# Memory projection first, squares of x summed by TensorE, no plain pair, and GpSimd for the lower parts of seven memory weight tiles

## The chip, the cores and the metric

The kernel runs on one core of a Trainium2 chip. The core's engines are TensorE (PE in the profile, its weight loads PEld), VectorE (DVE), ScalarE (ACT), GpSimd (POOL) and SyncE (SP), which here issues the DMA transfers. Each engine works through its own queue in order; semaphores tie the queues together. The metric is device time of one launch in microseconds, less is better.

## The reference

One layer of a decoder: an RMS norm of x, one combined projection, four groups of heads that mix over the tokens, and an output projection with a residual. 1,024 prompt tokens and 32 sample tokens are handled together (1,056 columns). Cut to what the change touches:

```python
def rmsnorm(x, g):
    xf = x.astype(jnp.float32)
    y = xf * lax.rsqrt(jnp.mean(xf * xf, axis=-1, keepdims=True) + EPS)
    return (y * g.astype(jnp.float32)).astype(x.dtype)

def memory_kv(mem, g_mem, w_mem_kv, g_mem_k):
    kv = rmsnorm(mem, g_mem) @ w_mem_kv          # 256 memory tokens, 2048 -> 1024
    k, v = jnp.split(kv, 2, axis=-1)
    k = rmsnorm(k.reshape(b, m, MEM_HEADS, MEM_HD), g_mem_k)
    return k, v.reshape(b, m, MEM_HEADS, MEM_HD)

hn = rmsnorm(x, g_norm)
proj = hn @ w_in                                 # group D's queries m_q among its columns
q = rmsnorm(m_q.reshape(b, L, MEM_HEADS, MEM_HD), g_mem_q)
s = jnp.einsum('blhd,bmhd->bhlm', q, mem_k) * (MEM_HD ** -0.5)
p = jax.nn.softmax(s, axis=-1)
o_mem = jnp.einsum('bhlm,bmhd->blhd', p, mem_v)
y_d = o_mem.reshape(b, L, GROUP_W) * jax.nn.silu(m_z)
```

## The kernel before

Everything is float32. A matmul with full accuracy is made of three matmuls on parts: an operand is split into an upper part (`wh`, `xh`: the value rounded to the type fp32r by a cast on ACT) and a lower part (`wl`, `xl`: value minus upper part, on DVE), and upper x upper, lower x upper and upper x lower are added in PSUM.

x lies transposed: 16 row tiles (k = 0 to 15) of 128 features by 1,056 tokens. The columns of `w_in` are 46 tiles of 128, taken two at a time as pairs. 44 of them (`ORDER`, L1708) are computed with one level of Strassen's scheme (`first_pair`, `second_pair`): seven products per pair, each of 24 matmuls of 264 columns, in two passes. Pass one works on row tiles 0 to 7, pass two on 8 to 15. The products are named by their x operand: B11, T2, B21, T1, T3, B22, T4 (`self.S`). Each operand is a difference or sum of four blocks of x (b11, b12 for row tiles 0 to 3, left and right half of the tokens; b21, b22 for 4 to 7), normalised first, split into two parts and kept for all pairs of the pass. `product` (L648) issues a product and asks `first_strands` (L432) for its operand as long as that does not stand; with every such step it also advances the projection of the memory (`memory`, L832) by one of its 16 steps. `make_weights` forms the seven weight operands of each pair on DVE and splits them. Results of pass one are written out and read back in pass two.

The remaining two tiles, Dq0 and Dq1 (queries of memory heads 0 and 1), are computed at the very start by `first_two` (L384) without that scheme: 16 x 2 x 3 x 3 = 288 matmuls of 352 columns on x times g, not yet normalised, since the norm is known only when all of x has come. `load_x` (L273) loads the 16 tiles, splits each (ACT L310, DVE L311), squares it on ACT (L289) and adds the squares up on DVE (L294). `row_norms` (L321) sums them over the features, takes the inverse root (`rsqrt`, some 13 small DVE operations in a chain) and spreads it over all partitions: R, by which the two tiles are multiplied (L415), and then x's blocks, together with g, in `first_strands` (`normal`, L440). GpSimd forms the lower parts of seven of the eight weight pieces of these tiles (L366).

`memory` loads the memory in two transfers and its weights in 16, splits them (ACT L881, DVE L882, two of 512 columns per step), and issues 12 matmuls of 512 columns per step (L902). Its last step feeds `memory_out`, which makes keys and values. The attention of a memory head (`d_head`, `d_unit`) is put into a queue of steps (`_Pipe`), of which `product` runs two ahead of each product's matmuls: heads 0 and 1 in pass one behind the first pair, 2 and 3 at the start of pass two.

Order on the engines is not the order of the source: the framework orders each engine's instructions, and a buffer of a pool is given again only when its last reader is done. So an engine's queue can wait for a buffer as well as for data.

Of the kernel before, what the change touches and what calls it, by code (L numbers as in the profile page):

```python
# [122 lines left out]
class _Step:  # L123
    def __init__(self, nc, tc, ctx, I, O):
# [148 lines left out]
    def load_x(self):  # L273
# [10 lines left out]
        self.x0, self.x0raw = block, raw  # L284

        def square(k, parts):
            sq = self.rtile("sq") if k < 8 else parts[2]
            for i, p in enumerate(parts[:2]):
                nc.scalar.activation(sq[:, i * H : i * H + H], p, AF.Square)  # L289
            i = int(k % 4 == 3)  # L290
            if self.acc[i] is None:
                self.acc[i] = sq
            else:
                nc.vector.tensor_tensor(self.acc[i], self.acc[i], sq, op=ALU.add)  # L294
        for k in range(KT):
            if k < 8:
                parts = [block(2 * (k // 4) + i, k % 4) for i in range(2)]
            else:
                xr = self.rtile("xr")
                parts = [xr[:, 0:H], xr[:, H:TOK], xr]  # L300
            if k < 8:
                for i in range(2):
                    nc.sync.dma_start(out=parts[i], in_=self.I["xT"][k, :, i * H : i * H + H])
            else:
                nc.sync.dma_start(out=parts[2], in_=self.I["xT"][k])
            hl = self.stile(F32R, "xhl")
            for i in range(2):
                h, l = (hl[:, x * TOK + i * H : x * TOK + i * H + H] for x in range(2))
                g = self.gn[:, k : k + 1]
                nc.scalar.activation(h, parts[i], AF.Copy, scale=g)  # L310
                nc.vector.scalar_tensor_tensor(l, parts[i], g, h.bitcast(F32), op0=ALU.mult,  # L311
                                               op1=ALU.subtract)
            self.xh[k], self.xl[k] = hl[:, 0:TOK], hl[:, TOK : 2 * TOK]
            if last:
                square(*last)
            last = k, parts
            if k == KT - 1:
                square(*last)
            yield k
# [1620 lines left out]
```

## Time and profile before

| what | value |
|---|---|
| median of 3 runs (lowest, highest) | 1568.07 us (1562.56, 1576.54) |
| the profiled execution | 1575.27 us |
| its span, first to last instruction | 1573.5 us |
| PE busy | 1530.4 us (97%) |
| DVE busy | 1105.2 us (70%) |
| ACT busy | 772.6 us (49%) |
| GpSimd busy | 23.3 us (1%) |
| mean granted TensorE clock | 0.985 |

The profile's tables give groups of instructions by line, engine, operation and tile names (output <- inputs), with shape and count, busy time, the mean duration of one in ns, and behind the bar the idle time ahead of them with what ended it. The timeline lists instructions in order of time, neighbours of one kind merged: start, duration, then in brackets how long the engine sat idle before and what it waited for. The chain of waits follows the work that ended last. Matmuls overlap: the duration of one is longer than the distance from its start to the next one's, so rates are taken from counts in a stretch.

### The profile page before, as it was taken

What the parts mean: (1) busy time and instruction counts of PE and PEld (TensorE: products, weight loads), DVE (VectorE), ACT (ScalarE), POOL (GpSimd) and SP (SyncE); (2) the same over time, 40 slices, a digit from 0 to 9 for tenths busy, and PEclk for the clock granted to TensorE, in tenths of its full rate; (3) what the DMA queues carried; (4) which work ended last, traced back from release to release, by engine and by line L of the source; (5) the groups of instructions that cost most, each with busy time, mean ns of one, the idle gap of its engine ahead of it and who ended that gap; (6) DMA issues with size and microseconds to landing.
All of it is one profiled execution on the core that took longest, in us unless ns stands there. A gap on an engine that the chain in (4) does not pass through costs nothing.

```text
span 1573.5 us, 30753 instructions
## 1 busy us (share of the span) xinstructions
PE 1530.4 (97%) x12194; PEld 1459.6 (93%) x12194; DVE 1105.2 (70%) x2283; ACT 772.6 (49%) x1620; POOL 23.3 (1%) x35
## 2 busy tenths in 40 slices
PE   7889999999999999999999999999998999999998
PEld 7668999999999999988998999999988999999998
DVE  8998645586555559665767776967779777596664
ACT  8466633322333336744468774645557443363332
POOL 3000000000000000000000000000000000000000
PEclk9899999999999999999999999999999999999999
DMA  7523222375332248158423333533437224587651
GB/s 272 193 92 109 69 103 94 142 267 193 109 110 100 95 148 308 62 144 298 139 78 84 109 90 121 173 123 90 167 119 244 82 104 168 188 288 267 209 203 63
DMA packets 102418, 236.77 MB, mean 150 GB/s; under 512 B 16516, under 2 KB 22532, under 8 KB 102276
## 3 DMA queue, kind: packets, MB, share of 16 engines
q1 hardware_dynamic: 102276, 234.82, 44.4%
q8 instruction: 96, 1.57, 0.4%
q14 instruction: 46, 0.38, 0.1%
HBM read 165.38 MB, written 69.41 MB: 149 GB/s over the span
## 4 chain that ended last, share of the span: by engine, by line
PE 75%; DVE 13%; ACT 5%; DMA 4%; issue 3%; SPq 0%; DVEq 0%; ACTq 0%
PE pj L668 64%; PE ms L902 2%; DVE wl L645 2%; DMA sx<-xs 1%; DVE s L430 1%; DVE xhl L311 1%; ACT wh L644 1%; ACT t L1280 1%; PE ms L1037 1%; DMA x<-in_xT 1%; ACT xhl L310 1%; DMA kc<-in_cache_mem_kT 1%; DVE t L1267 1%; PE ms L1313 1%; PE ms L1007 1%
## 5 line engine op out<-in xcount | busy, mean ns | idle before, releaser
L668 PE MATMUL pj<-s,wh 128*128 128x264 f32 x6720 | 1268.7, 288 | 7.6 <-ACT pj L751 5.5
L668 PEld LDWEIGHTS pj<-s,wh 128*128 128x128 f32 x6720 | 1055.5, 189 | 25.6 <-issue 12.7
L668 PE MATMUL pj<-s,wl 128*128 128x264 f32 x3360 | 960.3, 286 | 0.8 <-DVE wl L645 0.8
L668 PEld LDWEIGHTS pj<-s,wl 128*128 128x128 f32 x3360 | 636.7, 190 | 5.9 <-issue 4.1
L644 ACT CAST wh<-wr 128x512 fp32r<-128x512 f32 x300 | 186.3, 621 | 262.4 <-PE pj L668 248.3
L645 DVE TENSOR_TENSOR wl<-wr,wh 128x512 fp32r<-128x512 f32 x300 | 206.5, 688 | 119.8 <-ACT wh L644 119.4
L698 DVE TENSOR_TENSOR d<-d,pj 128x528 f32<-128x528 f32 x180 | 121.4, 701 | 102.1 <-PE pj L668 60.0
L644 ACT CAST wh<-ws 128x512 fp32r<-128x512 f32 x120 | 74.5, 621 | 93.9 <-PE pj L668 89.5
L645 DVE TENSOR_TENSOR wl<-ws,wh 128x512 fp32r<-128x512 f32 x120 | 82.5, 688 | 9.1 <-ACT wh L644 8.5
L751 ACT COPY pj<-d 128x528 f32<-128x528 f32 x120 | 72.5, 604 | 15.1 <-DVE u L761 5.5
L430 DVE TENSOR_TENSOR s<-sx,s 128x1056 fp32r<-128x1056 f32 x42 | 51.6, 1250 | 1.9 <-ACT s L429 1.9
L429 ACT CAST s<-sx 128x1056 fp32r<-128x1056 f32 x42 | 44.3, 1075 | 10.0 <-DMA sx<-xs 5.2
L772 DVE TENSOR_TENSOR d<-d,pj 128x528 f32<-128x528 f32 x30 | 21.1, 703 | 36.5 <-PE pj L668 36.5
L701 ACT COPY d<-pj 128x528 f32<-128x528 f32 x30 | 18.0, 599 | 55.1 <-PE pj L668 55.1
L707 ACT COPY d<-pj 128x528 f32<-128x528 f32 x30 | 18.0, 601 | 53.4 <-PE pj L668 53.4
L1280 ACT ACTIVATE t<-t,sm,sm 128x256 f32<-128x256 f32 (+1 forms) x64 | 37.1, 581 | 14.2 <-DVE sm L1272 14.2
L640 DVE TENSOR_TENSOR wr<-wr,ws 128x512 f32<-128x512 f32 x60 | 41.8, 697 | 1.0
L775 DVE TENSOR_TENSOR d<-u,pj 128x528 f32<-128x528 f32 x30 | 21.1, 703 | 30.1 <-PE pj L668 30.0
L626 DVE TENSOR_TENSOR ws<-wr,wr 128x512 f32<-128x512 f32 x60 | 41.3, 688 | 1.2
L636 DVE TENSOR_TENSOR wr<-wr,wr 128x512 f32<-128x512 f32 x60 | 41.3, 688 | 1.1
L627 DVE TENSOR_TENSOR ws<-ws,wr 128x512 f32<-128x512 f32 x60 | 41.3, 688 | 1.0
L778 DVE TENSOR_TENSOR d<-u,pj 128x528 f32<-128x528 f32 x30 | 21.1, 703 | 29.8 <-PE pj L668 29.6
(368 smaller groups left out, 1524.2 us busy)
## 6 DMA issues: line engine op xcount, KB each, us to landing
wr<-in_w_in SPq DMA_DIRECT2D x184, 256.0 KB
half_in<-d SPq DMA_DIRECT2D x44, 528.0 KB
d<-half_in SPq DMA_DIRECT2D x44, 528.0 KB
sx<-xs SPq DMA_DIRECT2D x42, 528.0 KB
wr<-in_w_out SPq DMA_DIRECT2D x64, 256.0 KB
x<-in_xT SPq DMA_DIRECT2D x24, 528.0 KB
xs<-t SPq DMA_DIRECT2D x36, 264.0 KB
half_out<-d SPq DMA_DIRECT2D x16, 528.0 KB
```

Source lines behind the costliest of these rows:

```text
L429: nc.scalar.copy(h[:, s], x)
L430: nc.vector.tensor_tensor(l[:, s], x, h[:, s].bitcast(F32), op=ALU.subtract)
L626: v.tensor_tensor(s1, r(1, 0), r(1, 1), op=ALU.add)
L627: v.tensor_tensor(s2, s1, r(0, 0), op=ALU.subtract)
L636: v.tensor_tensor(x, r(0, 0), x, op=ALU.subtract)
L640: v.tensor_tensor(x, x, self.wsum[n][1], op=ALU.subtract)
L644: nc.scalar.copy(wh, x)
L645: v.tensor_tensor(wl, x, wh.bitcast(F32), op=ALU.subtract)
L668: nc.tensor.matmul(ps[:, 512 * c : 512 * c + CG], w[:, ks], x[:, xs], start=(first and kk == 0 and n == 0), stop=(kk == 3 and n == 2), ski ...
L698: nc.vector.tensor_tensor(o, o, bank(ps), op=op)
L751: nc.scalar.copy(bank(ps), x)
L1280: nc.scalar.activation(ps[u][:, g, kts[0] : 2], ps[u][:, g, kts[0] : 2], AF.Exp, bias=mx[:, c : c + 1], scale=rq[:, 4 * m + c : 4 * m + c ...
```

## The change

The plain pair goes: `first_two`, `load_piece`, `split_piece` and `take` are removed, and Dq0 and Dq1 become the first pair of `ORDER`. `ORDER` has 46 tiles, so each pass has 23 pairs in place of 22. Their heads are handled at the start of pass two, ahead of heads 2 and 3, which takes two tiles less of buffer in pass one.

In its place `start` runs the first part of the memory's projection while x comes in: per memory step k = 0 to 7 two tiles of x are loaded and squared on ACT, and TensorE sums the squares of the two before (`sum_squares`: four matmuls of 32 rows in four strips of the array, accumulated over all 16 tiles in one bank). Tiles 0 to 7 of x are multiplied by g on DVE as they come; `normal` multiplies by R alone, with one wide operation per block. Three further memory steps stand between the parts of `row_norms`, and the last five go on as before between the steps of `first_strands`. The memory comes in four transfers, its weights two steps to a buffer, a step's 1,024 columns are split by one cast and one subtraction, and the subtraction of steps 9 to 15 is GpSimd's.

```diff
-    def first_two(self, evacs):
...
+    def square(self, k):
+        nc = self.nc
+        if k < 8:
+            sq = self.sq[k] = self.rtile("sq")
+            for i in range(2):
+                x = self.x0(2 * (k // 4) + i, k % 4)
+                nc.scalar.activation(sq[:, i * H : i * H + H], x, AF.Square)
+                nc.vector.tensor_scalar(x, x, self.gn[:, k : k + 1], None, op0=ALU.mult)
+        else:
+            nc.scalar.activation(self.sq[k], self.sq[k], AF.Square)
+
+    def sum_squares(self, k):
+        for j in range(4):
+            self.nc.tensor.matmul(self.sums[32 * j : 32 * j + 32, 0:CG], self.ones[:, 0:32],
+                                  self.sq[k][:, CG * j : CG * j + CG], start=(k == 0),
+                                  stop=(k == KT - 1), tile_position=(0, 32 * j))
+        self.sq[k] = None
...
+    def start(self, pool):
+        self.x_tiles()
+        self.mem_tiles = {}
+        self.mem = self.memory(pool)
+        bank = self.two()
+        self.sums, spare = bank[:, 0:512], bank[:, 512:1024]
...
+        def loads(k):
+            if k in (1, 4, 7):
+                self.load_mem(k // 3 + 1)
+            if k + 2 < KT:
+                self.load_mem_weights(k + 2)
+            for i in range(2):
+                if 2 * k + i < KT:
+                    self.load_x(2 * k + i)
+        for k in range(2):
+            loads(k)
+        for k in range(8):
+            if k + 2 < 8:
+                loads(k + 2)
+            next(self.mem)
+            for i in range(2):
+                self.square(2 * k + i)
+            if k:
+                for i in range(2):
+                    self.sum_squares(2 * k - 2 + i)
+        self.load_weights(0, ((0, 0), (1, 0), (1, 1), (0, 1)))
+        self.make_weights()
+        for i in range(2):
+            self.sum_squares(KT - 2 + i)
+        for _ in self.row_norms(spare):
+            next(self.mem)
...
         def normal(b):
-            for k in range(4 * (b // 2), 4 * (b // 2) + 4):
-                x = self.x0(b, k % 4)
-                h = slice(H * (b % 2), H * (b % 2) + H)
-                v.scalar_tensor_tensor(x, x, self.gn[:, k : k + 1], self.R[:, h], op0=ALU.mult,
-                                       op1=ALU.mult)
+            r = self.R[:, H * (b % 2) : H * (b % 2) + H].unsqueeze(1)
+            for x in self.x0raw[b] if b == 3 else [self.x0raw[b]]:
+                n = x.shape[1] // H
+                t = x.rearrange("p (k t) -> p k t", k=n)
+                v.tensor_tensor(t, t, r.to_broadcast([P, n, H]), op=ALU.mult)
...
         def weights(k):
...
+            nc.scalar.copy(wh, x)
+            (nc.gpsimd if k >= 9 else nc.vector).tensor_tensor(wl, x, wh.bitcast(F32), op=ALU.subtract)
...
-    ORDER = ["Dq2", "Dq3", "Ac0", "Ah0", "Az0", "Ab0", "Dz0", "Dz1", "Dz2", "Dz3",
+    ORDER = ["Dq0", "Dq1", "Dq2", "Dq3", "Ac0", "Ah0", "Az0", "Ab0", "Dz0", "Dz1", "Dz2", "Dz3",
...
-                self.second(hold(q))
-                for h in (2, 3):
-                    self.d_head(q[h], h)
+                for i in (0, 2):
+                    self.second(hold(q))
+                    for h in (i, i + 1):
+                        self.d_head(q[h], h)
```

What stands in the queues, at three places. GpSimd's queue in the first part of the program, before and after (`r` and `wl` before are lower parts of weight pieces; `wm` after holds both parts of a memory weight tile, `wr` is as loaded):

```order
L366 TENSOR_TENSOR r528_181<-wr17_140,r527_180 128x512
L247 AFFINE_SELECT own_1548<-own_1548 32x8
L366 TENSOR_TENSOR wl31_187<-wr26_178,wh30_186 128x512
L366 TENSOR_TENSOR r542_308<-wr29_184,r541_307 128x512
L366 TENSOR_TENSOR wl45_314<-wr40_305,wh44_313 128x512
L366 TENSOR_TENSOR r557_433<-wr43_311,r556_432 128x512
L366 TENSOR_TENSOR wl60_439<-wr55_430,wh59_438 128x512
L366 TENSOR_TENSOR r570_558<-wr58_436,r569_557 128x512
```

```order
L245 AFFINE_SELECT own_1095<-own_1095 32x8
L851 TENSOR_TENSOR wm69_488<-wr42_321,wm69_488 128x1024
L851 TENSOR_TENSOR wm78_541<-wr51_367,wm78_541 128x1024
L851 TENSOR_TENSOR wm82_580<-wr51_367,wm82_580 128x1024
L851 TENSOR_TENSOR wm87_602<-wr57_432,wm87_602 128x1024
L851 TENSOR_TENSOR wm92_627<-wr57_432,wm92_627 128x1024
L851 TENSOR_TENSOR wm97_676<-wr79_544,wm97_676 128x1024
L851 TENSOR_TENSOR wm98_714<-wr79_544,wm98_714 128x1024
```

Seven subtractions of 512 columns that stood along the plain pair have become seven of 1,024 for memory steps 9 to 15.

PE's queue around the transposes that spread R, before and after (`L337`, `L331`: these transposes; `xhl` x in two parts, `t`, `wh`, `wl` and `wm` memory weights, `r` memory in two parts):

```order
L406 MATMUL ms9_125<-xhl68_528,r569_557 128x352
L337 MATMUL pj6_122<-ident_94,sm74_609 128x128 [waits DVE_49]
L337 MATMUL pj6_122<-ident_94,sm74_609 128x128 x3
L337 MATMUL ms81_647<-ident_94,sm74_609 128x128 [waits PE_49]
L337 MATMUL ms81_647<-ident_94,sm74_609 128x128 x3
L337 MATMUL pj6_122<-ident_94,sm74_609 128x128 [waits DVE_49,Activation_49]
L406 MATMUL pj6_122<-xhl66_500,wh59_438 128x352 [waits Activation_49]
L406 MATMUL pj6_122<-xhl66_500,wl60_439 128x352
L406 MATMUL pj6_122<-xhl66_500,wh59_438 128x352
L406 MATMUL pj6_122<-xhl68_528,wh59_438 128x352
L406 MATMUL pj6_122<-xhl68_528,wl60_439 128x352
L406 MATMUL pj6_122<-xhl68_528,wh59_438 128x352
```

```order
L873 MATMUL ms13_154<-wm78_541,r567_482 128x512 [waits Pool_49]
...
L873 MATMUL ms16_157<-wm78_541,r568_483 128x512
L331 MATMUL pj8_128<-ident_94,sm70_507 128x128 [waits DVE_49]
L331 MATMUL pj8_128<-ident_94,sm70_507 128x128
L334 MATMUL pj8_128<-ident_94,sm71_508 128x8 [waits DVE_49]
L873 MATMUL ms13_154<-wm82_580,r567_482 128x512 [waits Activation_49]
L873 MATMUL ms13_154<-wm82_580,r567_482 128x512 [waits Pool_49]
L873 MATMUL ms13_154<-wm82_580,r568_483 128x512
L873 MATMUL ms15_156<-wm82_580,r567_482 128x512 x2
L331 MATMUL pj8_128<-ident_94,sm70_507 128x128 [waits Activation_49]
L331 MATMUL pj8_128<-ident_94,sm70_507 128x128
```

Before, the transposes stood in one block among the last matmuls of the plain pair, ahead of the memory's first step. After, step 10 of the memory stands ahead of them and step 11 among them, and both hold a wait for GpSimd (`Pool` in the brackets).

DVE's queue at the differences of x's blocks (before: b22 in `xb14` and `xb15`, b12 in `xb12`, b21 in `xb13`, b11 in `xb11`; after: `xb6` and `xb7`, `xb4`, `xb5`, `xb3`), before and after:

```order
L882 TENSOR_TENSOR t5145_931<-wm134_862,t5144_930 128x512 [waits DMAHW1_49]
L882 TENSOR_TENSOR wl147_935<-wm134_862,wh146_934 128x512 [waits Activation_49]
L444 SCALAR_TENSOR_TENSOR xb13_130<-xb13_130,consts_88,R2_118 128x528 x4
L882 TENSOR_TENSOR t5150_957<-wm139_904,t5149_956 128x512 [waits DMAHW2_49,PE_49,Activation_49]
L882 TENSOR_TENSOR wl152_961<-wm139_904,wh151_960 128x512 [waits Activation_49]
L470 TENSOR_TENSOR xb14_131<-xb14_131,xb12_129 128x1056 [waits DVE_49,PE_49]
L470 TENSOR_TENSOR xb15_132<-xb15_132,xb12_129 128x1056 [waits DVE_49,PE_49]
...
L472 TENSOR_TENSOR xb12_129<-xb12_129,xb11_128 128x2112
```

```order
L410 TENSOR_TENSOR xb5_125<-xb5_125,R2_118 128x2112
L839 TENSOR_TENSOR acc54_401<-acc54_401,mr28_236 128x256 [waits DVE_49]
L610 TENSOR_TENSOR wl132_932<-ws93_667,wh131_931 128x512 [waits PE_49,Activation_49]
L591 TENSOR_TENSOR ws162_1110<-wr63_466,wr144_1007 128x512 [waits DMAHW5_49,DMAHW0_49]
L592 TENSOR_TENSOR ws163_1111<-ws162_1110,wr62_464 128x512 [waits DMAHW7_49,DVE_49]
L601 TENSOR_TENSOR wr63_466<-wr62_464,wr63_466 128x512
L435 TENSOR_TENSOR xb6_126<-xb6_126,xb4_124 128x1056 [waits PE_49]
L435 TENSOR_TENSOR xb7_127<-xb7_127,xb4_124 128x1056 [waits PE_49]
L259 TENSOR_SCALAR sm103_752<-pj101_748 128x2 [waits PE_49]
L437 TENSOR_TENSOR xb4_124<-xb4_124,xb3_123 128x2112 [waits DVE_49]
```

The memory's subtractions (L882) and most of its other work have gone from between the strands' operations; b22 - b12 (L470 before, L435 after) waits for PE in both, and in the new queue of PE the matmuls that read b22 last (L463) stand behind the memory's step 15.

More of the change, by code (lines that the diff above doesn't have):

```diff
@@ L283, in block @@
             return t[:, k * H : k * H + H]
[L284 to L306, printed above, removed]
-            for i in range(2):
[L308 to L319, printed above, removed]
+        self.x0, self.x0raw, self.sq = block, raw, [None] * KT
@@ L326, in row_norms @@
-        for sums in self.token_sums(acc[:, 0:SEQ]):
-            pass
-        nc.tensor.matmul(spare[:, 0:2], acc[:, TOK - P : TOK], self.ones[:, 0:2], start=True,
-                         stop=True)
-        r = self.small(NB + 1, tag="rx")
-        self.rsqrt(r[:, 0:NB], sums, 1.0 / D_MODEL, EPS, NB)
-        self.rsqrt(r[:, NB : NB + 1], spare[:, 0:1], 1.0 / D_MODEL, EPS, 1)
-        for g in range(3):
-            ps = self.ps() if g == 1 else spare
-            blocks = list(range(4 * g, min(4 * g + 4, NB + 1)))
-            for i, n in enumerate(blocks):
-                nc.tensor.transpose(ps[:, i * P : i * P + P],
-                                    r[:, n : n + 1].to_broadcast([P, P]), self.ident)
-            if g < 2:
-                nc.scalar.copy(self.R[:, 512 * g : 512 * g + 512], ps)
-            else:
-                nc.scalar.copy(self.R[:, SEQ:TOK], ps[:, P - NS : P])
@@ new lines, in row_norms @@
+        nc.scalar.copy(rows, self.sums[:, 0:CG])
+        yield
+        for x in range(2):
+            nc.tensor.transpose(spare[:, x * P : x * P + P], rows[:, x * P : x * P + P],
+                                self.ident)
+        nc.tensor.transpose(spare[0:8, 2 * P : 3 * P], rows[:, 2 * P : CG], self.ident)
+        t = spare[:, 0 : 3 * P].rearrange("p (x j c) -> p x j c", x=3, j=4)[:, :, :, 0]
+        r, r8 = self.small(8, tag="rx"), self.small(4, tag="rx8")
+        self.rsqrt(r, t[:, 0:2], 1.0 / D_MODEL, EPS, 8)
@@ new lines, in row_norms @@
+        self.rsqrt(r8[0:8, :], t[0:8, 2], 1.0 / D_MODEL, EPS, 4)
+        yield
+        for j in range(4):
+            ps = spare if j % 2 else self.sums
+            for x in range(2):
+                nc.tensor.transpose(ps[:, x * P : x * P + P],
+                                    r[:, 4 * x + j : 4 * x + j + 1].to_broadcast([P, P]),
+                                    self.ident)
+            nc.tensor.transpose(ps[:, 2 * P : CG], r8[0:8, j : j + 1].to_broadcast([8, P]),
+                                self.ident[0:8, 0:8])
+            nc.scalar.copy(self.R[:, CG * j : CG * j + CG], ps[:, 0:CG])
@@ L451, in first_strands @@
         normal(1)
-        ps = self.two()
+        ps = self.sums
         def ranks(ks):
@@ L1716, in plan @@
         w = {t: I["w_in"][TILES.index(t)] for t in TILES}
-        for q in range(4):
-            self.pieces += [("w", w[t][:, 512 * q : 512 * q + 512]) for t in ("Dq0", "Dq1")]
         self.two_in = [self.ORDER[i : i + 2] for i in range(0, len(self.ORDER), 2)]
```

140 lines of the change are left out of this document (44 added, 96 removed).

## The prediction, made before the changed kernel was run

> **What bounds the kernel now.** I read first how busy each engine is in six stretches of the span, then what the vector engine (DVE) delivers in the second stretch, then the price of a pair of output tiles.
>
> ```profile
> 0.00:63.10 63.10, 51.57 (x303) 48.31 (x303) 54.88 (x93) 47.80 (x84) 15.29 (x18) 0.99 0.73 249
> 63.10:149.30 86.20, 79.22 (x435) 64.42 (x436) 79.38 (x119) 50.04 (x76) 0.20 (x1) 0.89 0.31 103
> ...
> 207.00:600.00 393.00, 390.64 (x3220) 385.51 (x3220) 236.48 (x352) 122.51 (x211) 0.00 (x0) 1.00 0.40 142
> 600.00:760.00 160.00, 154.29 (x1294) 142.85 (x1294) 108.53 (x204) 87.87 (x191) 3.95 (x9) 0.99 0.59 190
> ```
>
> Columns: stretch, its length, busy us (and instructions) of PE, PE's weight loads, DVE, ACT, GpSimd (POOL), granted clock, DMA share, GB/s. From 207 us on PE has 390.6 of 393 us and DVE 60%: TensorE bounds. Before 149 us it is otherwise: in the second stretch DVE has 79.4 of 86.2 us, and PE's 79.2 are stretched (clock 0.89). So the start is set by DVE, the rest by PE, and the change touches both: it adds two pairs to the PE-bound part and shortens the start. The forecast is the difference of these two.
>
> The start ends where the first pair's last product (T4) is read:
>
> ```profile
> 149.42 1.32 DVE L698 TENSOR_TENSOR d<-d,pj 128x528 f32<-128x528 f32 x2 [0.22 <-PE pj L668]
> 500.00:600.00 100.00, 100.00 (x826) 100.00 (x825) 1.00 0.40 140
> ```
>
> The first row says that PE ended T4 and went on with the second pair at about 149.3 us. The second counts L668's matmuls in 100 us of the PE-bound part: 121 ns each.
>
> **What the two new pairs cost.** Dq0 and Dq1 leave the plain pair (288 matmuls of 352 columns at the start) and become a pair of seven products in each of the two passes: 2 x 168 matmuls x 121 ns = 40.7 us, all on PE where PE bounds. Their DVE and ACT work (some 11 us of DVE per pair of 20.3 us) hides under PE, as for every pair in the third row above. Heads 0 and 1 of the memory attention move from the first pass to the second with the same matmuls: nothing, because DVE and ACT have 51 and 72 us free in the row 600:760; the queue of steps then still empties 0.7 of a pair before the stage drains. If that cover failed it would cost about 2 us.
>
> **When the new start ends.** I follow it in three parts.
>
> Part 1, to the last square of x. Loads stand in the order x, memory, memory weights mixed; up to the last tile of x they are x 8.65 MB, memory 2.1, ten weight tiles 5.2, constants 0.2: 16.2 MB.
>
> ```profile
> 0.00:6.00 6.00, 0.00 (x0) 0.00 (x0) 1.58 (x11) 1.89 (x5) 1.07 (x10) 1.00 0.56 165
> 6.00:14.00 8.00, 7.14 (x32) 6.30 (x33) 6.26 (x8) 7.96 (x14) 1.94 (x2) 1.00 1.03 364
> 14.00:26.00 12.00, 12.00 (x76) 12.00 (x75) 12.00 (x15) 12.00 (x22) 3.06 (x2) 1.00 1.05 399
> ...
> L881 ACT CAST t<-wm 128x512 fp32r<-128x512 f32 x16 | 9.9, 616 | 4.2 <-PE ms L902 3.6 <-DMA wm<-in_w_mem 0.5
> L289 ACT ACTIVATE sq<-xb 128x528 f32<-128x528 f32 x16 | 9.7, 630 | 0.0
> L848 ACT ACTIVATE r<-mr,consts 128x256 fp32r<-128x256 f32 x16 | 7.5, 502 | 7.5 <-PE ms L902 4.5 <-PE ms L406 2.9
> L429 ACT CAST s<-xb 128x1056 fp32r<-128x1056 f32 x4 | 4.1, 1075 | 0.0
> L856 ACT ACTIVATE mr<-mr 128x2048 f32<-128x2048 f32 x2 | 3.8, 1915 | 0.0
> ```
>
> The first 14 us moved 3.9 MB, the remaining 12.3 at 399 GB/s take 31 us: x is there at about 45 us. ACT is later: it waits in its order for x's ninth tile (10.3 MB, 30 us and the landing), and then has eight squares of 1,056 columns (1.0 us each net of the 0.08 by which neighbours overlap), four of 528, four casts of 1,024, two preparations of memory and memory's squares: 8.0 + 2.2 + 4.2 + 1.7 + 1.8 = 18 us, so 49.3 us. x's multiplication by g (16 times, each at most the 0.7 of L311 further down) adds at most 12 us to DVE's 20 there and costs nothing. SP issues a load in 0.48 us (next fence), 39 of them in 19 us. The last tiles of x reuse the buffers of squares that PE has summed by 36 us, with 2.6 MB still queued ahead of them, so that wait is hidden too.
>
> PE's share of this part, and the price of summing squares there, come from the nearest rows:
>
> ```profile
> 3.60 2.87 SPq L303 DMA_DIRECT2D xb<-in_xT  x6
> ...
> 94.15 1.97 PE L498 MATMUL pj<-xb,t 128*16 128x264 f32 x32
> 120.56 2.79 PE ms L902 x12
> 107.27 2.08 PE L902 MATMUL ms<-t,r 128*128 128x512 f32 x4 [3.90 <-DVE t L882]
> ```
>
> L498 has the form of the new sums (264 columns, four strips of PE), 16 of them in 1.97 us: 0.123 us each, 64 make 7.9 us. A step of the memory projection (12 matmuls of 512) takes 2.79 us. Nine steps and the sums are 33 us in 50, so I take them as hidden; the last four sums (0.5) and the ninth step, which stands ahead of the row norm's transposes, end at 53.2, the transposes at 53.7.
>
> Part 2, the row norm. Before it ran like this:
>
> ```profile
> 56.90 0.17 DVE L261 TENSOR_SCALAR sm<-ms 128x8 f32<-128x8 f32 x1 [0.47 <-PE ms L979]
> 60.92 0.24 DVE L270 SCALAR_TENSOR_TENSOR sm<-sm,sm 128x8 f32<-128x8 f32 x2
> 61.14 0.65 PE L337 MATMUL pj<-ident,sm 128*128 128x128 f32 x4 [2.02 <-DVE sm L270]
> 61.83 0.58 ACT L340 COPY R<-pj 128x512 f32<-128x512 f32 x1 [1.86 <-PE pj L337]
> ```
>
> DVE needed 4.3 us, with two weight additions inside. After it has four of them there: 4.3 + 1.2 + 0.2 = 5.7. But now GpSimd works beside it: its lower parts of k = 9 to 12 fill 50 to 66 us. What that costs DVE is the one price that decides, and the trace has it:
>
> ```profile
> 9.06 1.32 POOL L366 TENSOR_TENSOR r<-wr,r 128x512 fp32r<-128x512 f32 x1 [7.36 <-ACT r L362]
> 25.30 2.51 POOL L366 TENSOR_TENSOR r<-wr,r 128x512 fp32r<-128x512 f32 x1 [7.46 <-ACT r L362]
> 27.76 2.31 POOL L366 TENSOR_TENSOR wl<-wr,wh 128x512 fp32r<-128x512 f32 x1
> 30.04 1.75 POOL L366 TENSOR_TENSOR r<-wr,r 128x512 fp32r<-128x512 f32 x1
> 31.75 1.76 POOL L366 TENSOR_TENSOR wl<-wr,wh 128x512 fp32r<-128x512 f32 x1
> 9.65 3.34 DVE L311 SCALAR_TENSOR_TENSOR xhl<-xb,consts,xhl 128x528 fp32r<-128x528 f32 x4 [0.91 <-ACT xhl L310]
> 26.85 2.07 DVE L294 TENSOR_TENSOR sq<-sq,sq 128x1056 f32<-128x1056 f32 x1 [0.18 <-ACT sq L289]
> 28.84 5.91 DVE L311 SCALAR_TENSOR_TENSOR xhl<-xr,consts,xhl 128x528 fp32r<-128x528 f32 x4
> 38.37 1.44 DVE L311 SCALAR_TENSOR_TENSOR xhl<-xr,consts,xhl 128x528 fp32r<-128x528 f32 x2
> 39.73 1.24 DVE L294 TENSOR_TENSOR sq<-sq,xr 128x1056 f32<-128x1056 f32 x1
> ```
>
> Alone, DVE does one of 1,056 in 1.24 us and two of 528 in 1.44 us. While GpSimd had four operations of 512 columns from 25.3 us on, one and four took 2.07 + 5.91 us in place of 1.24 + 2.80: 4 us lost, 1 us for each, and GpSimd itself needed about 2 us for each. Beside the first, of 1.32 us, four took 3.34: half a microsecond lost. So I charge DVE 2.0 us for each new operation of 1,024, near the four rather than the one since DVE is as busy then, and GpSimd 4.1 us. Bounds: 0, and 2.6 (twice 1.32, all of GpSimd's shortest time). The subtraction saves DVE only 1.2 us (next rows). Three of the four fall into the row norm: 5.7 + 6 = 11.7, so 65.4; transposes, two copies and DVE's queue bring the first product with R to 67 us, against 66.5 before.
>
> [...]
>
> Part 3, from the first product with R to the last strand. Prices:
>
> ```profile
> L430 DVE TENSOR_TENSOR s<-xb,s 128x2112 fp32r<-128x2112 f32 x4 | 9.4, 2350 | 0.0
> L430 DVE TENSOR_TENSOR s<-xb,s 128x1056 fp32r<-128x1056 f32 x4 | 4.8, 1250 | 0.0
> L882 DVE TENSOR_TENSOR t<-wm,t 128x512 fp32r<-128x512 f32 x16 | 10.9, 683 | 0.0
> L849 DVE SCALAR_TENSOR_TENSOR r<-mr,consts,r 128x256 fp32r<-128x256 f32 x16 | 7.1, 477 | 0.0
> ```
>
> Net of the overlap of 0.08 us DVE has, up to the second half of T4: 8 of 2,112 (18.2 us), 14 of 1,056 (16.4), one of 1,024 (1.1), 11 of 512 or 528 (6.7), four of 256 (1.5) and 36 small ones (4.3): 48.2 us. With k = 13 to 15 on GpSimd, 6 us more: 67 + 54.2 = 121.2. The second pair's first weights are four short operations later: 124.0. One more wait may come: DVE's difference b22 - b12 waits for the gate rank's matmuls, which stand behind k = 15 on PE, which waits for GpSimd's last operation (86 us). At full clock PE is done at 91, when DVE arrives; PE restarts slowly after a gap (third row of the fence on PE: four in 2.08 us, where twelve take 2.79). I add 1.5: the second pair starts at 125.5.
>
> **Sum.** Before the second pair started at 149.3, after at 125.5: 23.8 us won. Two pairs: 40.7 lost. +17 us. The profiled execution took 1575.27 us (span 1573.5), so 1592 on its base; the median of the runs is 1568.07, so **1585 us**.
>
> **Rivals.** (a) Not slower: GpSimd's operations cost DVE nothing. For it: the operation at 9 us cost DVE half of the others; against it the four at 25 us. Then 12 us come back: +5 us, 1573. It decides below 1.8 us an operation, where six of them take the sum under 16 us. (b) PE's clock: the row 63.10:149.30 has 0.89, and the matmuls after the gap at 107 us ran at half speed. If PE stays slow in part 1, its 33 us become 66 in 50, the sums of squares end up to 8 us late and everything behind them: +25, 1593. [...] (c) Faster by 1%: the start would have to end at 92 us; DVE's 48 us from R on leave R by 44, before x has landed. Only if pairs cost less than 121 ns a matmul; no row shows that.
>
> **Chances.** The forecast case (+10 to +24: 1578 to 1592) 0.60; (a) 0.17; (b) 0.15; (c) 0.04; small sums of errors 0.04. A measurement of this kernel can tell about 1% (16 us) from no change. Of the forecast case 0.36 lies beyond +16. Slower: 0.36 + 0.15 + 0.02 = 0.53; same: 0.24 + 0.17 + 0.02 = 0.43; faster 0.04. Range 1572 to 1598.
>
> **What would show it.** Right: the first pair's T4 read near 122 us, R near 66, DVE operations beside GpSimd's stretched by 2 us each, two pairs more at 20.3 us in the PE-bound part, 600 to 760 without new waits. Wrong: DVE unstretched beside GpSimd (a); sums of squares ending after 55 us with a clock under 0.8 (b); R much later because loads wait for buffers; the heads' steps reaching past the drain.

## The result, and the profile after

| what | value |
|---|---|
| median of the changed kernel (lowest, highest), 4 runs | 1594.51 us (1589.60, 1595.71) |
| the kernel before on the same chip, 4 runs | 1569.13 us (1562.56, 1576.54) |
| ratio, 95% interval | 1.0155 [1.0114, 1.0196] |
| the same two kernels in a later set, 5 and 23 runs | 1588.79 and 1571.01 us, ratio 1.0133 [1.0110, 1.0155] |
| span of the profiled execution, after and before | 1593.9 and 1573.5 us |

The change makes the kernel slower by 1.3 to 1.6%, 18 to 25 us; the two profiles differ by 20.4. The forecast was 17 us, and it named this side.

The stretches of the changed kernel, cut where its first pair ends (columns as in the prediction: stretch, length, busy us of PE, PE's weight loads, DVE, ACT and GpSimd, granted clock, DMA share, GB/s):

```profile
0.00:63.10 63.10, 45.10 (x263) 29.48 (x263) 38.22 (x79) 41.19 (x61) 9.10 (x15) 0.97 0.90 338
63.10:130.70 67.60, 50.02 (x318) 39.96 (x319) 62.38 (x91) 33.12 (x56) 12.29 (x9) 0.85 0.08 24
207.00:600.00 393.00, 388.55 (x3202) 383.38 (x3201) 245.05 (x357) 132.11 (x221) 0.00 (x0) 1.00 0.43 155
600.00:760.00 160.00, 155.04 (x1257) 140.32 (x1257) 91.93 (x222) 94.39 (x231) 4.14 (x9) 0.99 0.40 127
```

DVE is still the fullest engine of the start's second part (62.4 of 67.6 us, the time in which it is held by GpSimd included), TensorE that of the rest. The start is shorter: T4 of the first pair is read at 130.7 us, where it was 149.4. Here is that read on DVE's timeline of the changed kernel:

```profile
130.72 0.69 DVE L663 TENSOR_TENSOR d<-d,pj 128x528 f32<-128x528 f32 x1
```

From there on the first product of each pair of pass two is a marker (ACT copies it out of PSUM). First the kernel before, then the changed one; the last row of each is the first pair behind the memory heads:

```profile
615.25 0.59 ACT L757 COPY u<-pj 128x528 f32<-128x528 f32 x1
...
756.20 0.60 ACT L757 COPY u<-pj 128x528 f32<-128x528 f32 x1 [0.55 <-PE pj L668]
```

```profile
595.20 0.59 ACT L722 COPY u<-pj 128x528 f32<-128x528 f32 x1
617.39 0.60 ACT L722 COPY u<-pj 128x528 f32<-128x528 f32 x1 [1.28 <-PE pj L633]
...
776.88 0.60 ACT L722 COPY u<-pj 128x528 f32<-128x528 f32 x1 [0.55 <-PE pj L633]
```

The account of the two profiles is this: start -18.6 us (130.7 against 149.3). Pass one from there to its end -1.4 (465.95 before, 595.20 - 130.7 = 464.5 after), although it has a pair more, because heads 0 and 1 have left it. The stretch with the memory heads 181.7 against 141.0, +40.7: the other new pair and the two heads. Everything behind: 20.4 - 20.7 = -0.3.

### The profile page after: what moved, and what is told of

It is laid out like the page before. It is cut to its first block, busy times and chain, and to the rows that moved or that the text cites. A ratio compares the mean times of both kernels' runs of the same rounds, so it can differ in the third digit from the quotient of the medians.

```text
span 1593.9 us, 31009 instructions
## 1 busy us (share of the span) xinstructions
PE 1533.3 (96%) x12364; PEld 1455.8 (91%) x12364; DVE 1089.1 (68%) x2243; ACT 758.4 (48%) x1582; POOL 28.6 (2%) x35
## 4 chain that ended last, share of the span: by engine, by line
PE 77%; DVE 11%; DMA 5%; ACT 4%; issue 2%; SPq 0%; ACTq 0%; DVEq 0%
PE pj L633 67%; DVE wl L610 2%; DVE s L395 1%; DMA x<-in_xT 1%; DMA xb<-in_xT 1%; PE ms L873 1%; PE ms L978 1%; ACT wh L609 1%; ACT t L1251 1%; PE ms L1008 1%; DVE xb L410 1%; DMA out_conv_s<-sm 1%; DVE t L1238 1%; PE ms L1284 1%; DMA xr<-in_xT 1%
## 5 line engine op out<-in xcount | busy, mean ns | idle before, releaser
L633 PE MATMUL pj<-s,wh 128*128 128x264 f32 x6944 | 1312.1, 288 | 18.0 <-ACT s L394 8.2
L633 PEld LDWEIGHTS pj<-s,wh 128*128 128x128 f32 x6944 | 1090.5, 189 | 38.0 <-issue 14.3
L633 PE MATMUL pj<-s,wl 128*128 128x264 f32 x3472 | 991.5, 286 | 0.8 <-DVE wl L610 0.8
L633 PEld LDWEIGHTS pj<-s,wl 128*128 128x128 f32 x3472 | 658.1, 190 | 4.4 <-issue 2.9
L609 ACT CAST wh<-wr 128x512 fp32r<-128x512 f32 x310 | 192.4, 621 | 269.5 <-PE pj L633 259.2
L610 DVE TENSOR_TENSOR wl<-wr,wh 128x512 fp32r<-128x512 f32 x310 | 215.2, 694 | 129.7 <-ACT wh L609 129.4
L663 DVE TENSOR_TENSOR d<-d,pj 128x528 f32<-128x528 f32 x186 | 125.5, 700 | 109.5 <-PE pj L633 60.8
L610 DVE TENSOR_TENSOR wl<-ws,wh 128x512 fp32r<-128x512 f32 x124 | 85.3, 688 | 9.5 <-ACT wh L609 8.8
L873 PE MATMUL ms<-wm,r 128*128 128x512 f32 x192 | 52.2, 421 | 9.5 <-ACT wm L850 9.2
L873 PEld LDWEIGHTS ms<-wm,r 128*128 128x128 f32 x192 | 36.6, 199 | 22.3 <-ACT wm L850 11.2
L666 ACT COPY d<-pj 128x528 f32<-128x528 f32 x31 | 18.6, 600 | 62.2 <-PE pj L633 62.2
L672 ACT COPY d<-pj 128x528 f32<-128x528 f32 x31 | 18.6, 601 | 57.3 <-PE pj L633 57.2
```

What stands on the lines that cost most here:

```text
L609: nc.scalar.copy(wh, x)
L610: v.tensor_tensor(wl, x, wh.bitcast(F32), op=ALU.subtract)
L633: nc.tensor.matmul(ps[:, 512 * c : 512 * c + CG], w[:, ks], x[:, xs], start=(first and kk == 0 and n == 0), stop=(kk == 3 and n == 2), ski ...
L663: nc.vector.tensor_tensor(o, o, bank(ps), op=op)
L873: nc.tensor.matmul(ps[t][c], a[:, ts], b, start=(k == 0 and i == 0), stop=(k == KT - 1 and i == 2))
```

## The experiments

Twelve runs in three sets, each set on one chip with the kernel before. "Second pair" is the time at which ACT starts to copy the second pair's first product; in the changed kernel and its variants that is 24 matmuls (2.9 us) behind the end of the first pair, so an expectation that says "first pair ends" or "second pair starts at 124" is met at 127 there. In variants of the kernel before, ACT comes to that copy some 2 us later than it could, since it works at the memory's keys (in before T4 is read at 149.4 us, and 24 matmuls on it is 152.3); compare each family with its own first row (the expectations have these times less 2.9 us too: 151.5 for the 154.4 of before). Each time comes from one profile. The changed kernel was run again in the second set (expected: ratio 1.0155 within 0.003, first pair's end at 130 to 133 us; measured: 1.0133 and 131.3). It and pair_less have the changed kernel's start, and their second pairs come at 133.6, 134.2 and 135.7, so a difference of 2 us in this column may be chance.

| kernel | ratio to before, 95% interval | multiplication by R begins, us | second pair, us |
|---|---|---|---|
| before | 1 | 66.5 | 154.4 |
| changed (two sets) | 1.0155 [1.0114, 1.0196]; 1.0133 [1.0110, 1.0155] | 69.3; 69.6 | 133.6; 134.2 |
| all_vector | 1.0089 [1.0073, 1.0106] | 67.8 | 127.4 |
| early_gpsimd | 1.0093 [1.0075, 1.0112] | 69.7 | 129.5 |
| cut_gpsimd | 1.0104 [1.0083, 1.0125] | 66.8 | 133.8 |
| norm_first | 1.0128 [1.0107, 1.0150] | 60.8 | 132.4 |
| vector_norm_first | 1.0072 [1.0049, 1.0096] | 60.8 | 123.4 |
| warm | 1.0070 [1.0045, 1.0094] | 68.6 | 127.0 |
| pair_less | 0.9983 [0.9969, 0.9997] | 70.4 | 135.7 |
| before_sums | 1.0040 [1.0024, 1.0056] | 66.3 | 154.9 |
| before_vector | 0.9970 [0.9954, 0.9987] | 62.6 | 148.6 |
| sums_early | 0.9971 [0.9957, 0.9985] | 60.1 | 149.7 |
| sums_early_vector | 0.9982 [0.9965, 0.9999] | 59.2 | 148.8 |

**GpSimd undone.** In `weights`:

```diff
-            (nc.gpsimd if k >= 9 else nc.vector).tensor_tensor(wl, x, wh.bitcast(F32), op=ALU.subtract)
+            nc.vector.tensor_tensor(wl, x, wh.bitcast(F32), op=ALU.subtract)
```

> The changed kernel with the lower parts of memory steps 9 to 15 on DVE again; GpSimd does nothing in the start. Theory A (a GpSimd operation of 1,024 takes DVE's place for its whole length, 2.2 us and more, where DVE itself needs 1.15 us for the same work): DVE's operations in 50 to 90 us lose their stretching (8 columns in 2.3 us become 0.15 us, 1,056 columns in 3.4 become 1.24), seven operations of 1.15 come to DVE, the multiplication by R begins about 4 us earlier (65 in place of 69.3 us), the first pair ends about 7 us earlier (123 to 125 in place of 130.7 us), and the kernel takes 6 to 9 us less than the changed one (1586 to 1589 against 1594.5). Theory B (GpSimd costs DVE little, and the start is late for PE's order and the ranks): DVE only gets 8 us more work, the first pair ends at 136 to 139 us and the kernel takes 1600 to 1603.

Theory A holds. First the seven subtractions in the changed kernel, then DVE's in this one (ns: least, median, most):

```profile
L851 POOL TENSOR_TENSOR wm<-wr,wm x7: 2342/2519/3433, 49.8 to 83.0; 128x1024 fp32r<-128x1024 f32 x7
```

```profile
L851 DVE TENSOR_TENSOR wm<-wr,wm x16: 1206/1220/1226, 8.6 to 79.8; 128x1024 fp32r<-128x1024 f32 x16
```

DVE does in 1.22 us what takes GpSimd 2.34 or more. And while GpSimd worked, DVE stood for most of the time (14.3 of 19.0 us, counted below): this is DVE's timeline of the changed kernel around GpSimd's operations (those began at 49.8, 52.6, 60.2, about 62.5, and three from 77.0 on):

```profile
50.43 2.42 DVE L828 SCALAR_TENSOR_TENSOR r<-mr,consts,r 128x256 fp32r<-128x256 f32 x2 [2.21 <-ACT r L827]
53.06 2.59 DVE L610 TENSOR_TENSOR wl<-wr,wh 128x512 fp32r<-128x512 f32 x1 [0.21 <-ACT wh L609]
...
60.23 2.32 DVE L266 TENSOR_TENSOR sm<-sm 128x8 f32<-128x8 f32 x1
62.48 0.14 DVE L268 SCALAR_TENSOR_TENSOR sm<-sm,sm 8x4 f32<-8x4 f32 x1
62.59 2.27 DVE L267 TENSOR_TENSOR sm<-sm,sm 128x8 f32<-128x8 f32 x1
...
77.27 6.84 DVE L410 TENSOR_TENSOR xb<-xb,R 128x1056 f32<-128x1056 f32 x2
84.04 3.43 DVE L837 TENSOR_TENSOR mr<-mr 128x1024 f32<-128x1024 f32 x1
```

And two of these lines on DVE's timeline without GpSimd (all_vector):

```profile
76.89 2.42 DVE L410 TENSOR_TENSOR xb<-xb,R 128x1056 f32<-128x1056 f32 x2
79.23 0.68 DVE L837 TENSOR_TENSOR mr<-mr 128x512 f32<-128x512 f32 x1
```

An operation on eight columns, 0.15 us alone, takes 2.32: as long as one GpSimd operation. Counted line by line (0.88 us for the pair of L828, 0.69 for L610, 0.15 each for the two small ones, 2.42 for the pair of L410, 1.23 for L837) the loss is 1.5 + 1.9 + 2.2 + 2.1 + 4.4 + 2.2 = 14.3 us for seven, 2.05 each. Put on DVE they cost 7 x 1.22 = 8.5, so the second pair should come 5.8 us earlier; it comes 6.2 earlier. The time falls by 0.4 to 0.7% of the kernel before (7 to 10 us by the two measurements of the changed kernel). R itself gained 1.5 us, not 4: the memory's matmuls stand between the transposes in PE's queue (below), and behind them DVE took up an operation of the memory (L837) first, which waited for ACT.

**GpSimd where DVE has time.** `nc.gpsimd if 2 <= k < 9 else nc.vector`:

> The changed kernel with GpSimd's seven subtractions moved to memory steps 2 to 8, in the stretch from 10 to 50 us in which DVE has half of its time free; steps 9 to 15 are DVE's. Theory A (a GpSimd operation takes DVE's place for its length wherever it stands, but that costs time only where DVE is the bound): DVE's operations beside it are stretched by up to 2.3 us in 10 to 50 us, yet the row norm begins at the same 54 to 56 us, and the first pair ends within 2 us of the kernel without GpSimd (124.5): time 1580 to 1585. Theory B (a GpSimd operation costs the whole kernel about 1 to 1.5 us wherever it stands, since x's and the memory's steps wait for it): the first pair ends at 129 us or later, 1590 or more.

Theory A, at its edge: the second pair is 2.0 us later than without GpSimd and 4.1 earlier than in the changed kernel; the times of this run and of all_vector can't be told apart (1.0093 and 1.0089). One part of the expectation failed: the row norm began at 57.0 us, not at 54 to 56 (54.9 in all_vector). GpSimd's last two subtractions ran from 47.8 to 52.5 us, and ACT's copy of the sums of squares (L316), with which the norm begins, came at 53.9 us, against 51.2 in the changed kernel. So most of the price is paid where DVE is the bound (6.2 us at the second pair), and little of it elsewhere (2.0). It falls on one-input operations too: the multiplications of x by g took up to 2.64 us beside GpSimd, and at most 0.50 in the changed kernel, where nothing stands beside them:

```profile
L298 DVE TENSOR_SCALAR xb<-xb,consts x16: 482/496/2640, 11.2 to 36.4; 128x528 f32<-128x528 f32 x16
```

**GpSimd's operations cut into four.**

```diff
+            n = 256 if k >= 9 else 1024
+            for c in range(0, 1024, n):
+                s = slice(c, c + n)
+                (nc.gpsimd if k >= 9 else nc.vector).tensor_tensor(
+                    wl[:, s], x[:, s], wh[:, s].bitcast(F32), op=ALU.subtract)
```

> The changed kernel with each of GpSimd's seven subtractions of 1,024 columns cut into four of 256. Theory A (DVE waits for the end of the GpSimd instruction that runs, gets one instruction in, and waits for the next): the longest stretch of a short DVE operation falls from 2.3 us to 0.6 to 0.8, but the sum that DVE loses beside GpSimd stays (about 2 us for each 1,024 columns) as long as GpSimd has instructions left, and the first pair ends at 129 to 133 us as before. Theory B (DVE comes ahead of GpSimd at every break): DVE loses less than half, first pair by 127. Theory C (each GpSimd instruction has its own fixed price): GpSimd needs over 3.5 us for 1,024 columns and the first pair ends after 134.

Theory A by its main signs. The operation on eight columns now waits for a quarter, and the quarters themselves wait for DVE (DVE's row, then GpSimd's group):

```profile
60.35 0.70 DVE L266 TENSOR_TENSOR sm<-sm 128x8 f32<-128x8 f32 x1
```

```profile
L854 POOL TENSOR_TENSOR wm<-wr,wm x28: 722/944/2832, 49.5 to 90.7; 128x256 fp32r<-128x256 f32 x28
```

The second pair comes at 133.8, as in the changed kernel (133.6): cutting changes who waits when, and hardly how long both need together. One sign of theory C is met too: four of the seven subtractions take GpSimd over 3.5 us, the last three 17.4 us in all in place of 9.4. A fixed price is not the main reason, since four quarters at their least are 2.9 us against 2.34 for the whole; the rest fits GpSimd's waiting for its turn. And the first pair's end after 134, which C forecast, did not come. The ratio of 1.0104 is lower than 1.0133, but the intervals overlap and the start gives no reason for it.

**The memory's steps out of the row norm.** `for _ in self.row_norms(spare): pass` in place of `next(self.mem)` per part, first with GpSimd, then without:

> The changed kernel with the three memory steps between the parts of the row norm taken out of there; they run later, between the strands. Theory A (the memory's matmuls that stand among the transposes of R are 2 to 3 us of the delay of R): R is multiplied from about 66.5 us in place of 69.3, and the GpSimd operations of steps 11 to 13, now later, move their 2.3 us each from the row norm to the strands, so the first pair ends at 128 to 130 us against 130.7: 1 to 3 us less in all. Theory B (PE's queue there is not on the path, DVE's total work is): R earlier, but the first pair ends within 1 us of 130.7. Theory C: the memory's three steps are then late for what follows them (keys and values of the memory, the last strand), and the first pair ends at 134 us or later.

> The changed kernel without GpSimd and without memory steps between the parts of the row norm. Theory A (DVE's whole work is the bound, and an earlier R only fills DVE's idle time, which in the kernel without GpSimd is 3.6 of 40 us between 50 and 90): R is multiplied from 60 to 62 us in place of 67.8, but the first pair ends only 1 to 3 us earlier than 124.5. Theory B (R's delay passes through in full): the first pair ends at 117 to 119. Theory C: the memory's late steps hold the ranks or the last strand, 125 or later.

R comes 8.5 us earlier with GpSimd, more than the 2.8 expected: three of its operations leave the row norm too. They meet the strands instead. DVE's timeline of norm_first:

```profile
60.80 4.62 DVE L410 TENSOR_TENSOR xb<-xb,R 128x2112 f32<-128x2112 f32 x2
65.34 2.35 DVE L395 TENSOR_TENSOR s<-xb,s 128x2112 fp32r<-128x2112 f32 x1
67.61 11.25 DVE L410 TENSOR_TENSOR xb<-xb,R 128x1056 f32<-128x1056 f32 x3
```

The row at 67.61 stands for three operations that need 1.2 + 1.2 + 2.35 us alone. So of 8.5 us only 1.2 reach the second pair. That is theory A of the first in its sum, but 1.2 us is less than the 2 us that may be chance, so its theory B is not out. Without GpSimd the same edit brings R 7.0 us earlier and the second pair 4.0: more than the 1 to 3 of theory A, less than the 5.5 to 7.5 of theory B. Part of R's delay was on the path, and both theories were too simple. The times of all_vector and vector_norm_first (1.0089 and 1.0072) can't be told apart.

**A warm TensorE.** Behind the last matmul of the memory:

```diff
+        x = self.S[B11][0]
+        for _ in range(40):
+            nc.tensor.matmul(rp[:, 512 : 512 + CG], x[:, 0:P], x[:, 0:CG], start=True, stop=True)
```

> The changed kernel without GpSimd, with 40 extra matmuls of 264 columns (their result unused) in TensorE's gap ahead of the first pair's second product, to keep its clock up. In the kernel without GpSimd TensorE stands idle for 7.1 us there, and then needs 0.165 us for a matmul for 5 to 7 us in place of 0.121; the chain of waits runs over 44 of these matmuls. Theory A (the cold restart is on the path, the term of 1.5 us of the prediction): granted clock in 90 to 125 us above 0.95 in place of 0.80, first pair ends 2 to 3 us earlier than 124.5. Theory B (the splits on DVE behind it are the bound anyway): clock up, first pair within 0.7 us of 124.5.

The stretch from 90 to 125 us, first of the kernel without GpSimd, then of this one:

```profile
90.00:125.00 35.00, 23.62 (x162) 22.42 (x163) 32.30 (x67) 21.61 (x42) 1.14 (x5) 0.80 0.14 46
```

```profile
90.00:125.00 35.00, 28.74 (x230) 26.45 (x222) 32.39 (x65) 21.39 (x41) 1.56 (x5) 0.95 0.15 46
```

The clock is up from 0.80 to 0.95, DVE's busy time is unchanged, and the second pair comes 0.5 us earlier. By these numbers it is theory B, but the run does not settle it. The extra matmuls ended at 98.6 us and the clock fell again at 102 (to 0.51, last section), so the 44 matmuls on the chain of waits got only part of the gain. Here they are without and with the extra matmuls (start, time, engine, line and count; at 121 ns each they would take 5.3 us):

```profile
102.10 7.78 PE pj L633 x44
```

```profile
102.67 6.88 PE pj L633 x44
```

Besides, R's first multiplication came 0.8 us later than in all_vector, though the two programs are the same up to there; counted from it, the second pair comes 1.3 us earlier. And ACT reached the memory's keys in another order. What a cold TensorE costs the start is open.

**The price of a pair.** The second pass of Dq0, Dq1 left out, its first-pass results read back (cut to the main part):

```diff
+                    if i:
+                        self.second(hold(q))
+                    else:
+                        self.nth += 1
+                        q += [self.rtile("d") for _ in range(2)]
+                        for t, src in zip(q, self.kept(self.two_in[0])):
+                            self.nc.sync.dma_start(out=t, in_=src)
```

> The changed kernel without the second pass of the pair Dq0, Dq1: the first pass's results are read back and used as they are, so that the queries of memory heads 0 and 1 lack row tiles 8 to 15 of x. It prices one pair of output tiles by itself. Theory (one pair is 168 matmuls of 121 ns where TensorE bounds, nothing else): 20.3 us less than the changed kernel, so 1574 against 1594.5, with 1 to 2 us given back if the steps of heads 0 and 1, which now begin one pair earlier with less matmul work beside them, reach TensorE. Rival (a pair costs less than its matmuls since its work fills holes): 10 to 17 us less.

From the second pair to the first pair behind the memory heads it takes 757.8 - 135.7 = 622.1 us, the changed kernel 776.9 - 133.6 = 643.3: 21.2 us less. The time falls by 1.50% (from 1.0133) or 1.72% (from 1.0155), 24 to 27 us, with 4 to 7 us of uncertainty: 20.3 is at the edge of that. The same stretch lasts 639.0 to 645.5 us, 641.8 in the mean, in the eight profiles that have all pairs, so the pair is worth 19.7 us by the mean and 16.9 to 23.4 by single profiles. That fits the 20.3, and the rival of 10 to 17 reaches only the lowest of them. This is the marker's row in its trace:

```profile
757.80 0.60 ACT L722 COPY u<-pj 128x528 f32<-128x528 f32 x1 [0.55 <-PE pj L633]
```

**One part of the change alone.** The kernel before with the squares summed by TensorE, the plain pair kept (`sum_squares` of the change, called behind each tile's matmuls):

```diff
-            if self.acc[i] is None:
-                self.acc[i] = sq
-            else:
-                nc.vector.tensor_tensor(self.acc[i], self.acc[i], sq, op=ALU.add)
+            self.sq[k] = sq
...
+                for n in {0: (0, 1), 12: (13, 14, 15)}.get(k, (k + 1,) if k < 12 else ()):
+                    self.sum_squares(n)
```

> The kernel before with one part of the change alone: the squares of x are summed by TensorE (64 small matmuls), the 15 additions of squares on DVE (1.17 us each) and the final one go; the plain pair stays. Theory A (in 14 to 53 us ACT is nearly as full as DVE, 2.53 us for each of 16 tiles of x, so it becomes the pace; and PE gets 8 us more work): squares end near 51 us as before, R's first multiplication near 63.5 us against 66.5, the second pair starts about 3 us earlier (146), time within 0.4% of the kernel before. Theory B (DVE alone sets the pace up to 63 us): R by 57 us, second pair by 140 us, time 1558 to 1561. Theory C (PE in order behind late squares delays the plain pair): second pair after 150 us, time 1570 or more.

Neither of the first two but C: 0.4% slower. DVE's row at the norm shows why nothing was won:

```profile
62.30 0.22 DVE L261 TENSOR_SCALAR sm<-ms 128x8 f32<-128x8 f32 x2 [7.26 <-PE ms L337]
```

DVE, freed of 18 us (the 14 additions of L294 took 18.2 us in before), waits 7.3 us for TensorE, whose queue holds the last sums behind the plain pair's thirteenth tile and the row norm's transposes behind its fourteenth. The second pair came only 0.5 us later than in the kernel before, so the start does not explain the 0.4%, 6 us; where the rest lies was not found. The wait is a matter of order, so the sums and the norm were put ahead of the twelfth:

```diff
+                if k == 11:
+                    for n in range(12, KT):
+                        self.sum_squares(n)
+                    norms = self.row_norms()
+                    next(norms)
```

> The kernel before with the sums of squares on TensorE, as in before_sums, but the last four tiles' sums and the row norm put ahead of the plain pair's twelfth tile in TensorE's order, not behind its thirteenth. In before_sums TensorE worked without a gap from 20 to 68 us and the transposes came only at 61.8 us while the last square was ready near 50 and DVE stood idle for 10 us. Theory A (only TensorE's order held R there): sums end near 52 us, the multiplication by R begins at 57 to 59 us in place of 66, DVE's 83 us to the end of the first pair begin that much earlier, the second pair starts at 143 to 146 in place of 151.5, and the kernel takes 1561 to 1565 where before takes 1570. Theory B (TensorE's own work bounds the start: the sums and the plain pair add up whatever the order): R earlier, but the second pair still at 150 to 152 and the time 1569 to 1576.

R at 60.1 (expected 57 to 59), the second pair at 149.7, or 146.7 as the expectation counts it (143 to 146), 4.7 us earlier than before, time 0.9971: faster than the kernel before, theory A with a gain just below its range in the start and at its end in the time. What stops it is probably TensorE, which is now nearly full; the run with both edits below fits that. The first 150 us as one stretch, of before and then of this one:

```profile
0.00:150.00 150.00, 131.49 (x744) 113.43 (x745) 134.85 (x213) 98.54 (x160) 15.49 (x19) 0.93 0.48 164
```

```profile
0.00:150.00 150.00, 140.05 (x899) 115.98 (x899) 117.81 (x215) 102.56 (x181) 12.13 (x23) 1.00 0.50 172
```

DVE has 17 us less to do, TensorE is busy 140 of 150.

**GpSimd undone in the kernel before**, alone and with the last edit (`split_piece`):

```diff
-        eng = nc.gpsimd if 0 < n < 8 else nc.vector
-        eng.tensor_tensor(wl, wr, wh.bitcast(F32), op=ALU.subtract)
+        nc.vector.tensor_tensor(wl, wr, wh.bitcast(F32), op=ALU.subtract)
```

> The kernel before with its seven GpSimd subtractions of 512 columns on DVE. In the trace of before they cost DVE about 6.5 us (0.5 beside the first, 1.0 beside the second, 4 beside the four from 25 us on, 1.0 beside the last), while DVE does one in 0.61 us, 4.3 us in all. Theory A (same rule as in the changed kernel): DVE gains 2 us by 55 us, the multiplication by R starts 1 to 3 us earlier than 66.5, time 1566 to 1569 where before stands at 1570. Theory B (GpSimd's 512-column operations are worth their place): R 4 us later, time 1574.

> The kernel before with both edits that helped it: sums of squares on TensorE with the row norm early in TensorE's order, and the seven GpSimd subtractions on DVE. Theory A (a GpSimd operation costs only where DVE is the bound; with the sums on TensorE that engine is the bound from 20 to 70 us and DVE has 20 of 50 us free): the gains don't add, the second pair starts within 1.5 us of sums_early (146.7), time 0.997 of before within 0.0015. Theory B (each edit takes its own wait away): second pair at 141 to 143, time 0.993 to 0.994.

Alone: R 3.9 us earlier, the second pair 5.8, time 0.9970 [0.9954, 0.9987]. Theory A, with a gain above its 1 to 3 us; what the excess is was not taken apart. Together the two edits don't add (0.9982 [0.9965, 0.9999], second pair 0.9 us from sums_early): that is theory A, by which DVE's lost time costs little with TensorE as the bound there (with both edits TensorE is busy 55.5 of the first 63 us, DVE 39.2). The versions that beat both kernels are thus sums_early and before_vector, each by 0.3%, and the two together by 0.2%; all keep the plain pair.

## Why the prediction was right, and where it was off

- **Two pairs at 40.7 us: right.** By the markers they and the moved heads are -1.4 + 40.7 = +39.3. The markers of before show the two pairs with heads 0 and 1 beside them 36.2 and 24.9 us long in place of 20.4, 20.3 us of the heads' work in all, so the heads leave pass one with 20.3 and come back in the other stretch; two pairs at 20.4 make 40.8, and 1.5 us were won. From T4's read to the first pair behind the heads, the eight profiles of the changed kernel and its variants with all pairs last 644.7 us in the mean (641.8 to 648.3), the five of the kernel before and its variants 606.6 (605.3 to 607.5): 38.0 us more. So the term is right to within 3 us. pair_less measures one pair at 19.7 us by the mean, 21.2 against the first profile.
- **Moved heads at nothing: right.** I allowed a loss of up to 2 us; the two profiles have a gain of 1.5, which is within chance by the spread just given. TensorE is busy 155.0 of 160 us in 600 to 760, where it was 154.3.
- **Part 1 right, rival (b) wrong.** The sums of squares ended at 51.1 us and the ninth memory step at 54.1, at a clock of 0.97 over the first 63 us. I had put that step's end at 53.2, though the terms I gave (49.3 + 0.5 + 2.8) make 52.6; the transposes came from 53.9 to 54.4, forecast 53.7. PE's timeline:

```profile
50.01 1.10 PE L306 MATMUL pj<-xr,ones 128*32 128x264 f32 x16
51.04 3.02 PE L873 MATMUL ms<-wm,r 128*128 128x512 f32 x12
53.91 0.38 PE L320 MATMUL pj<-ident,t 128*128 128x128 f32 x2
```

  Rival (b) had 1593 us, close to the median of 1594.5, by a mechanism that did not occur. A time that fits is no proof.
- **GpSimd's price, the step that decided: right.** I charged DVE 2.0 us an operation, the trace shows 2.05 in the mean. So the row norm ended where I had it, at 65.3 us (forecast 65.4). Rival (a), nothing, is out by all_vector, cut_gpsimd and the rows, with 2.32 us for eight columns.
- **The start's end at 125.5 us: wrong by 5.2, the term that was mis-sized.** I compare with 125.5, the end of my sum; the sign "T4 read near 122 us" in the prediction does not agree with that sum. R's first multiplication was put at 67, and came at 69.3, all of it behind the row norm. My sentence "transposes, two copies and DVE's queue bring the first product with R to 67 us" left out that the memory's matmuls stand between the transposes in PE's queue, though the order showed it. The chain of waits of the changed kernel runs through them:

```profile
65.13 0.68 PE pj L331 x2
65.81 0.20 PE pj L334
66.01 2.43 PE ms L873 x5
68.44 0.26 PE pj L331 x2
```

  Five matmuls take 2.43 us, 0.49 each, where twelve take 3.0 at full clock (0.25 each, clock 1.00 in 51 to 54 us): PE had stood idle for 5.2 us, and its granted clock was 0.50 from 65 to 68 us. From R to the last split I had 54.2 us, measured 57.7 (69.3 to 127.0). GpSimd's three operations there are 0.6 of the 3.5 (6.6 for 6.0). The rest lies in waits, which a sum of DVE's durations doesn't have. I had DVE as the bound up to the last strand, but from 108.5 us on the chain runs over TensorE and ACT. First come 44 matmuls behind a gap of 7.2 us, 2.2 us longer than at 121 ns each, and then the memory's keys. The same chain:

```profile
108.50 7.56 PE pj L633 x44
...
118.17 0.59 ACT t L890
118.76 0.58 ACT vm L904
119.34 1.16 ACT t L895 x8
120.50 0.58 ACT t L890
121.08 0.58 ACT vm L904
121.66 0.27 ACT t L895 x2
121.93 0.10 issue
122.03 0.79 ACT t L895 x5
122.81 0.50 ACT d L679
```

  ACT does the keys for 4.6 us, and T1's copy out of PSUM (L679), for which TensorE waits, stands behind them in its queue. TensorE's own idle time there is 1.5 us:

```profile
123.35 0.39 PE L633 MATMUL pj<-s,wh 128*128 128x264 f32 x1 [1.49 <-ACT d L679]
```

  How much of the 3.5 us each of the two waits cost was not tried. From the last split to T4's end it took 0.6 us less than I had put there (3.7 for 2.8 + 1.5). As to R, vector_norm_first takes the memory's matmuls from between the transposes: R came 7 us earlier, and 4 of them reached the second pair.
- **The wait for the ranks and a cold TensorE, 1.5 us: not seen where I put it.** In the changed kernel DVE went on to b22 - b12 without a wait for the ranks. The slow restart is on the chain later, at T2 (the 2.2 us above); warm took 0.9 us off its 44 matmuls, and what the rest costs is open.
- **Sum.** -18.6 (forecast -23.8) + 39.3 (40.7) - 0.3 = 20.4, forecast 16.9. The first median was 25 above that of before and the second 18; the profile lies between. What of the two medians' difference is chance I can't say: the part behind the heads' first pair, which no edit touched, lasts from 811.6 to 818.8 us in the fourteen profiles. The direction and the two large terms were forecast by the mechanism that the runs show; that the total is within 4 us owes something to chance, since the start was off by 5.2 one way and pairs and rest by 1.7 the other.

## What to carry to other kernels

- A helper engine is priced by what it takes from the engine it helps: here GpSimd saved DVE 1.22 us an operation and cost it 2.05. Look for it in the durations of DVE's shortest instructions, where a stall of 2.3 us can't hide.
- Here the same work cost less in an engine's gaps than where that engine bounds: the plain pair filled TensorE's holes in the start, and its removal, with the rest of the change, shortened the start by only 18.6 us; as Strassen pairs where TensorE bounds it cost some 40.
- A part of a change that is good alone can be held by order: the sums on TensorE lost 0.4% with the last of them and the norm behind the plain pair's late tiles in its queue, and won 0.3% ahead of them.
